# The first projection's accumulating transfers issued at once, the order of the start, and a shorter tail, in a one-core encoder layer

## The chip, the cores and the metric

The kernel runs on one core of a Trainium2 chip. The metric is the device time of one execution in microseconds (us); the time before is the median of three runs.

TensorE (PE in the profile) multiplies and transposes, VectorE (DVE), ScalarE (ACT) and GpSimd (POOL) work element by element, and SyncE (SP) only issues DMA transfers. ACT and POOL issue some as well. Each engine runs its own instructions in order, and semaphores order the engines among each other. PSUM, into which PE writes, has eight banks here, taken from one pool (`ps`).

## The reference, cut to what matters

One layer of a bidirectional encoder, in float32, for one sequence of 512 tokens of 2048 numbers:

```python
h = rmsnorm(x, attn_norm_w[l])
proj = h @ w_in[l]
aq, ak, av, gq, gk, gv, gr, glr = jnp.split(proj, split_idx, axis=-1)
attn = mixture_of_dilations(heads(aq), heads(ak), heads(av), rel_bias_table)
gla_out = gated_linear_attention(gq, gk, gv, glr, gr)       # in both directions
x = x + jnp.concatenate([attn, gla_out], axis=-1) @ w_out[l]
h = rmsnorm(x, ffn_norm_w[l])
x = x + (jax.nn.silu(h @ w_gate[l]) * (h @ w_up[l])) @ w_down[l]
return rmsnorm(x, final_norm_w)
```

`w_in` has 6176 columns, of which the first 2048 give the attention's queries and keys (`aq`, `ak`); the hidden width of the last part is 5632. The final `rmsnorm` multiplies each row by the reciprocal root of its mean square plus 1e-6, and by a weight for each column.

## The kernel before, in words

**Arithmetic.** Every float32 operand is cut into a high part (a cast to fp32r, on ACT) and a low part (the rest, a subtraction on DVE). A product is three matmuls into one bank: high by high, high by low, low by high. The large projections save one in eight block products by a scheme of seven products over sums of blocks of the weights and of the activations; DVE makes these sums (L1399 to L1401), ACT casts them (L1412) and DVE takes the rests (L1417).

**Order of the work.** `run` at the end goes through a list of jobs, each a group of matmuls with a stream of weights (`st`) that is loaded by SP (L209), cast (L237, ACT) and subtracted (L218, DVE). Job 0 begins with `start0` (L1124 to L1159 and around): SP issues the first parts of x and of the weights; ACT issues the attention norm's weights (`wrow1`, L433) and then the identity (`idn`, L434); PE spins on a zero tile (`spin`, L1124), transposes the norm weights by the identity (L1154), spins twice, transposes the first block of x (`prep(0)`, L450, followed by ACT L455), and spins once. The first real matmuls are L346 to L348. Two jobs compute the attention's values. Then `Front.run` computes queries and keys, and the next job computes the gated part's q and k (its first matmul is L337). The attention itself, the rest of the gated part, `w_out`, the feed-forward part (`Feed`), `Down` and the last rows (`finish`) follow.

**Front.** `Front` (L1636 to L1691) has 8 units of 256 output columns, alternately of queries and keys; a unit has 4 pieces of 512 rows of weights, so 32 pieces in all. For each piece it loads weights ahead (`load`), casts and subtracts (`split`), makes the sums of the pieces one and two ahead (`sums`), and runs the seven products on PE (`products`, L1494 and L1508), each into a bank of its own: seven banks for a unit of the eight there are. After the fourth piece `evac7` (L1524 to L1561) reads the seven banks and combines them: ACT copies (L1534 to L1542) into narrow buffers `t`, `r1`, `r2`, `r3` and the result `c`, and DVE adds and subtracts (L1528, L1529). The function is a generator. Up to its first `yield` it runs in the unit's last piece; the rest is put into a queue (`urgent`) from which `run_urgent` takes one step per piece. So one piece later come a wide add (L1552, recorded under L1528) and the four transfers on POOL's queue that add `r1`, `r2` and both halves of `r3` into `c` in memory (L1554 to L1557); the third waits for the first two. Three pieces after that (seven for the last but one unit) `finish` scales `c` by the tokens' reciprocal norms (L1651, DVE) and POOL stores it to `qkd` (L1652). The last unit's scaling is held back (`self.late`).

**Buffers.** Wide buffers (`s4`, 33 of them, names with b) and narrow ones (`s2`, 36, names with a) are handed out first in, first out. Whoever writes into a buffer waits until its last reader, a DMA included, is done. While Front runs, few are free: five narrow ones, all of which `evac7` takes, so that each unit gets the same five in the same roles.

**Around the seam.** In the last unit, Front loads the next job's first weights (`st.load`), after its second piece issues the eight transfers that read the first queries and keys back (`read_qk(0)`, L568, on POOL) and after its third the loads of the gated part's small operands. The next job's weights are cast (L237) when that job starts, behind the last unit's copies on ACT.

**Tail.** `last` (L2061 to L2094) handles the last 512 columns of the last 128 rows in two halves of 256: matmuls, the residual add (L2073, DVE), the sum of squares (L2077, ACT) and the product with the final weight (L2078, DVE). Behind the first half, DVE sums the four earlier partial sums of squares (L2080, L2081). Behind the second, ACT computes logarithm and exponential for the reciprocal root (L2082, L2083), DVE corrects it by one Newton step (L2084 to L2088), and DVE and ACT scale the four output tiles (L2092, L2089), each of which is written by a DMA (L2093) on SP's or ACT's queue.

Of the kernel before, what the change touches and what calls it, by code (L numbers as in the profile page):

```python
# [18 lines left out]
AF = mybir.ActivationFunctionType  # L19
OP = mybir.AluOpType  # L20
# [3 lines left out]
P = 128  # L24
D = 2048
# [6 lines left out]
EPS = 1e-6  # L32
# [80 lines left out]
def put(*slots):  # L113
    for s in slots:
        if s.home is not None:
            s.home.free.append(s.i)


def layer(nc, tc, x, attn_norm_w, w_in, rel_table, gw_f, gb_f, gw_b, gb_b, gla_norm_w, w_out,
# [3 lines left out]
    w_gate, w_up, w_down, out = w_gate[0], w_up[0], w_down[0], out[0]  # L123
# [3 lines left out]
    with tc.manual_schedule(), \  # L127
# [303 lines left out]
        dve.memset(warm, 0.0)  # L431
        xt[0] = [s4.get(F32, [P, 4, 256]) for _ in range(2)]
        act.dma_start(out=wrow1, in_=attn_norm_w[0].rearrange("(r c) -> r c", c=P))  # L433
        act.dma_start(out=idn, in_=c_idn)  # L434

# [75 lines left out]

        def squares(c, t, tiles, ss):
            junk = s2.get()
            act.activation(junk.t, tiles[t].t, AF.Square, accum_out=ss[:, t * 4 + c:t * 4 + c + 1])
            put(junk)
# [611 lines left out]
        def start0():  # L1127
# [27 lines left out]
            dve.tensor_copy(wcol[:, 0:16], b.t)  # L1155
            put(b)
            spin(2)
            prep(0)
            spin(1)  # L1159

# [262 lines left out]
        class Feed(Blocks):  # L1423
# [5 lines left out]
            PRODUCTS = (("R", 0, "B11"), ("Z", 2, "T2"), ("Z", 1, "T1"), ("Z", 0, "T3"), ("R", 2, "B21"),  # L1429
                        ("R", 1, "T4"), ("Z", 3, "B22"))  # L1430
            NARROW = ((0, 0), (1, 0), (2, 0), (2, 1), (0, 1), (3, 1), (3, 0))

# [91 lines left out]
            def evac7(self, u, banks):  # L1524
# [25 lines left out]
                put(*banks)  # L1550
                yield
                add(c[:, 256:768], c[:, 256:768], v.t)  # L1552
# [5 lines left out]
                put(r1, r2, r3)  # L1558
                for _ in range(3 if u < len(self.units) - 2 else 7):
                    yield  # L1560
# [75 lines left out]
        class Front(Feed):  # L1636


            def __init__(self):
# [21 lines left out]
            def run(self):  # L1661
                banks = {}
                for i, (u, q) in enumerate(self.seq):
# [9 lines left out]
                    while 2 * q + 1 not in xi:  # L1673
                        run_side(1)
                    self.products(i, banks[u])
                    if u == len(self.units) - 1:
# [4 lines left out]
                        if q == 2:  # L1681
                            gla_operands()
                    done = None
                    if q == self.per - 1:
                        if u == len(self.units) - 1:
                            s2.free.rotate(14)
                        done = self.evac7(u, banks.pop(u))
                        next(done)
                    run_urgent()
                    if done:  # L1690
                        urgent.append(done)  # L1691

# [334 lines left out]

        def load_wf():
            for c in range(4):
                t = s2.get()  # L2030
                src = final_norm_w[c * 512:(c + 1) * 512].rearrange("(o c) -> o c", o=1)
                pool.dma_start(out=t.t, in_=src.to_broadcast([P, 512]))
                wf.append(t)

        def finish():
# [25 lines left out]
            def last(ys):  # L2061

                t, c = 3, 3
                m, r = scr[0][:, 0:1], scr[1][:, 0:1]
                pre, q = scr[0][:, 1:2], scr[1][:, 1:2]
                sm, sq = sum2[:, t:t + 1], scr[0][:, 2:3]
                junk = s2.get()
                x_ = x1[c][t].t
                for h in range(2):
# [5 lines left out]
                    put(b)  # L2075
                    acc = (ss2[:, 4 * t + 3:4 * t + 4], sq)[h]
                    act.activation(junk.t[:, cols], x_[:, cols], AF.Square, accum_out=acc)  # L2077
                    dve.tensor_tensor(ys[c].t[:, cols], x_[:, cols], wf[c].t[:, cols], op=OP.mult)  # L2078
                    if h == 0:
                        dve.tensor_reduce(sm, ss2[:, 4 * t:4 * t + 4], op=OP.add, axis=mybir.AxisListType.X)  # L2080
                        dve.tensor_scalar(pre, sm, 1.0 / D, EPS, op0=OP.mult, op1=OP.add)  # L2081
                act.activation(q, sq, AF.Ln, scale=1.0 / D, bias=pre)  # L2082
                act.activation(r, q, AF.Exp, scale=-0.5)  # L2083
                dve.scalar_tensor_tensor(m, sq, 1.0 / D, pre, op0=OP.mult, op1=OP.add)  # L2084
                dve.scalar_tensor_tensor(q, r, r, m, op0=OP.mult, op1=OP.mult)
                dve.tensor_scalar(q, q, -0.5, 1.5, op0=OP.mult, op1=OP.add)
                rs = rstdf[:, t:t + 1]
                dve.tensor_tensor(rs, r, q, op=OP.mult)  # L2088
                act.activation(ys[2].t, ys[2].t, AF.Copy, scale=rs)  # L2089
                for c in (0, 2, 1, 3):  # L2090
                    if c != 2:
                        dve.tensor_scalar(ys[c].t, ys[c].t, rs, None, op0=OP.mult)  # L2092
                    (act if c >= 2 else sp).dma_start(out=out[t * P:(t + 1) * P, c * 512:(c + 1) * 512], in_=ys[c].t)  # L2093
                put(junk)  # L2094

            def run():
                for t in range(4):
                    ys = []
                    for c in range(4):
# [7 lines left out]
                        residual(c, t, b)  # L2107
                        squares(c, t, x1[c], ss2)
                        if t == 3:
# [53 lines left out]
```

## Time and profile before

| | us |
|---|---|
| Median of three runs | 2182.22 (2181.07 to 2182.69) |
| The profiled execution's own time | 2181.53 |
| Its span | 2179.8 |
| TensorE busy | 2161.3 (99%) |
| VectorE busy | 1771.2 (81%) |
| ScalarE busy | 1195.9 (55%) |
| GpSimd busy | 338.9 (16%) |

The page gives busy times, the chain of work that ended last and the costliest groups of instructions. Views of the trace show single stretches: a timeline has start and duration of an instruction (or of several of one kind in a row, with their count), the engine, the line, what it writes and reads, and in square brackets how long the engine stood idle before it and what released it. A landing time is what passes from the issue of a transfer until its data is there. Times in rows count from the span's start. Front runs from about 107 us to 267 us, its units 19 to 21 us each.

### The profile page before, as it was taken

What the parts mean: (1) busy time and instruction counts of PE and PEld (TensorE: products, weight loads), DVE (VectorE), ACT (ScalarE), POOL (GpSimd) and SP (SyncE); (2) the same over time, 40 slices, a digit from 0 to 9 for tenths busy, and PEclk for the clock granted to TensorE, in tenths of its full rate; (3) what the DMA queues carried; (4) which work ended last, traced back from release to release, by engine and by line L of the source; (5) the groups of instructions that cost most, each with busy time, mean ns of one, the idle gap of its engine ahead of it and who ended that gap; (6) DMA issues with size and microseconds to landing.
All of it is one profiled execution on the core that took longest, in us unless ns stands there. A gap on an engine that the chain in (4) does not pass through costs nothing.

```text
span 2179.8 us, 34563 instructions
## 1 busy us (share of the span) xinstructions
PE 2161.3 (99%) x12618; PEld 1904.2 (87%) x12618; DVE 1771.2 (81%) x3073; ACT 1195.9 (55%) x2189; POOL 338.9 (16%) x474
## 2 busy tenths in 40 slices
PE   9999999999999999999999999999999999999998
PEld 7888878888888888988888888888888899999986
DVE  5698767776766557899999898998999888898885
ACT  7445456776554335555555555555555655555562
POOL 0011231110011110012212122121221220021300
PEclk9999999999999999999999999999999999999999
DMA  6376774543337873377767777677776975576982
GB/s 201 125 187 173 189 226 141 176 140 111 105 103 270 288 247 107 120 182 177 198 176 183 180 176 196 178 181 182 177 196 176 263 201 182 181 183 157 283 304 78
DMA packets 256856, 397.81 MB, mean 183 GB/s; under 512 B 18925, under 2 KB 154269, under 8 KB 256686
## 3 DMA queue, kind: packets, MB, share of 16 engines
q1 hardware_dynamic: 201262, 272.43, 39.3%
q0 software_dynamic: 54960, 122.58, 24.9%
q8 instruction: 99, 1.62, 0.3%
q14 instruction: 71, 0.58, 0.1%
q10 hardware_dynamic: 464, 0.60, 0.1%
HBM read 285.37 MB, written 64.29 MB: 160 GB/s over the span
## 4 chain that ended last, share of the span: by engine, by line
PE 89%; issue 6%; DMA 2%; DVE 2%; ACT 1%; POOL 0%; ACTq 0%; DVEq 0%; POOLq 0%
PE ps L1508 27%; PE ps L1494 14%; PE ps L346 6%; PE ps L347 6%; PE ps L348 6%; PE ps L1864 5%; PE ps L1865 5%; PE ps L1863 5%; PE ps L339 3%; PE ps L337 3%; PE ps L338 3%; DMA b<-a 2%; PE ps L662 1%; PE ps L1086 1%; PE ps L630 1%
## 5 line engine op out<-in xcount | busy, mean ns | idle before, releaser
L1412 ACT CAST b<-b 128x768 fp32r<-128x768 f32 (+1 forms) x537 | 489.4, 945 | 338.5 <-DVE b L1417 151.2
L1417 DVE TENSOR_TENSOR b<-b,b 128x768 fp32r<-128x768 f32 (+1 forms) x537 | 563.6, 1084 | 32.9 <-ACT b L1412 21.5
L1508 PE MATMUL ps<-b,b 128*128 128x512 f32 x1552 | 451.4, 393 | 0.4 <-ACT b L1412 0.2
L1508 PE MATMUL ps<-a,b 128*128 128x512 f32 x1248 | 366.0, 394 | 3.3 <-DVE b L1528 3.3
L1508 PEld LDWEIGHTS ps<-b,b 128*128 128x128 f32 x1552 | 263.5, 188 | 30.6 <-ACT b L1412 0.7
L1494 PEld LDWEIGHTS ps<-b,b 128*128 128x128 f32 x1552 | 253.1, 190 | 35.8
L1494 PE MATMUL ps<-b,b 128*128 128x256 f32 x1552 | 275.6, 280 | 0.0
L1494 PEld LDWEIGHTS ps<-a,b 128*128 128x128 f32 x1248 | 208.1, 189 | 34.1 <-DVE b L1417 0.5
L1508 PEld LDWEIGHTS ps<-a,b 128*128 128x128 f32 x1248 | 207.2, 189 | 23.3 <-ACT a L1540 4.0
L1494 PE MATMUL ps<-a,b 128*128 128x256 f32 x1248 | 223.8, 281 | 0.0
L1399 DVE TENSOR_TENSOR b<-b 128x512 f32<-128x512 f32 x244 | 167.2, 685 | 17.8 <-DMA b<-in_w_down_dram 7.0
L1864 PE MATMUL ps<-b,b 128*128 128x256 f32 x624 | 176.8, 283 | 0.0
L1863 PE MATMUL ps<-b,b 128*128 128x256 f32 x624 | 176.8, 283 | 0.0
L1865 PE MATMUL ps<-b,b 128*128 128x256 f32 x624 | 176.8, 283 | 0.0
L346 PE MATMUL ps<-b,b 128*128 128x512 f32 x352 | 139.8, 397 | 0.3 <-ACT b L455 0.3
L348 PE MATMUL ps<-b,b 128*128 128x512 f32 x352 | 137.6, 391 | 0.0
L347 PE MATMUL ps<-b,b 128*128 128x512 f32 x352 | 137.5, 391 | 0.0
L1865 PEld LDWEIGHTS ps<-b,b 128*128 128x128 f32 x624 | 119.9, 192 | 0.0
L1863 PEld LDWEIGHTS ps<-b,b 128*128 128x128 f32 x624 | 119.9, 192 | 0.0
L1864 PEld LDWEIGHTS ps<-b,b 128*128 128x128 f32 x624 | 119.9, 192 | 0.0
L218 DVE TENSOR_TENSOR b<-b,b 128x512 fp32r<-128x512 f32 x143 | 95.9, 686 | 26.1 <-ACT b L237 26.0
L1401 DVE TENSOR_TENSOR b<-b,b 128x256 f32<-128x256 f32 x244 | 103.8, 425 | 8.4
(296 smaller groups left out, 4351.7 us busy)
## 6 DMA issues: line engine op xcount, KB each, us to landing
b<-in_w_gate_dram SPq DMA_DIRECT2D x109, 512.0 KB, 3.9
b<-in_w_up_dram SPq DMA_DIRECT2D x88, 512.0 KB, 3.7
b<-in_w_down_dram SPq DMA_DIRECT2D x88, 512.0 KB, 5.9
b<-in_w_in_dram SPq DMA_DIRECT2D x78, 512.0 KB, 4.0
b<-a POOLq DMA_DIRECT2D x150, 256.0 KB, 4.6
b<-in_w_out_dram SPq DMA_DIRECT2D x32, 512.0 KB, 6.6
gd<-b POOLq DMA_DIRECT2D x22, 512.0 KB, 3.9
b<-gd SPq DMA_DIRECT2D x22, 512.0 KB, 5.6
```

What stands on the lines that cost most here:

```text
L346: mm(o, xh.t[:, c], wh.t[:, w], start=first and not on, stop=False, skip_group_check=on)
L347: mm(o, xh.t[:, c], wl.t[:, w], start=False, stop=False, skip_group_check=on)
L348: mm(o, xl.t[:, c], wh.t[:, w], start=False, stop=last, skip_group_check=on)
L1399: dve.tensor_tensor(s_[:, :, 0:2], r[:, :, 1:3], r[:, :, 0:1].to_broadcast(shape), op=OP.add)
L1401: dve.tensor_tensor(s_[:, :, 3], s_[:, :, 2], r[:, :, 3], op=OP.add)
L1412: act.copy(o, src)
L1417: dve.tensor_tensor(o, src, h, op=OP.subtract)
L1494: mm(o, wl, xh, start=False, stop=end, skip_group_check=True)
L1508: mm(o.rearrange("p (s t) -> p s t", s=2), wh, x_, start=first and p == 0, stop=False, skip_group_check=True)
L1863: mm(o, xh[:, t], wh, start=first and h == 0, stop=False, skip_group_check=True)
L1864: mm(o, xh[:, t], wl, start=False, stop=False, skip_group_check=True)
L1865: mm(o, xl[:, t], wh, start=False, stop=last, skip_group_check=True)
```

## The change

At the start ACT issues the identity ahead of the norm weights, and one spin stands before the first transposes instead of two, two behind them instead of one.

In Front (`early = True`; `Feed` keeps its order) the wide add and the four accumulating transfers follow the copies and adds of `evac7` at once, without a step in between. The scaling and the store of a unit come when piece `min(i + 6, 31)` is reached, where i is the unit's last piece; the last unit's stays held back. In the last piece of the last unit, before its products are issued, `st.split` casts the next job's first two weight tiles and takes their rests, so that these stand on ACT ahead of the last unit's copies.

In the tail the sums of squares of the last rows go to one row of a small tile that also holds the constant for epsilon (set by a POOL memset in `load_wf`). ACT sums them with an accumulating copy behind the first half. Behind the second half, DVE multiplies and sums in one instruction, ACT computes logarithm and exponential with the total as bias, the Newton step ends with two factors instead of their product, and DVE scales all four tiles with both, their writes going to SP and ACT in turn.

```diff
         dve.memset(warm, 0.0)
         xt[0] = [s4.get(F32, [P, 4, 256]) for _ in range(2)]
+        act.dma_start(out=idn, in_=c_idn)
         act.dma_start(out=wrow1, in_=attn_norm_w[0].rearrange("(r c) -> r c", c=P))
-        act.dma_start(out=idn, in_=c_idn)
 
         rb = {}
         hT = {}
...
             pe.transpose(b.t, wrow1, idn[0:16, 0:16])
             dve.tensor_copy(wcol[:, 0:16], b.t)
             put(b)
+            spin(1)
+            prep(0)
             spin(2)
-            prep(0)
-            spin(1)
 
         def between0(i, b):
             if i == 0 and b == 1:
...
+            early = False
...
                 add(c[:, 768:1024], t1[:, a], v.t[:, z])
                 add(c[:, a], m2[:, a], t.t[:, a])
                 put(*banks)
-                yield
+                if not self.early:
+                    yield
                 add(c[:, 256:768], c[:, 256:768], v.t)
                 put(t, v)
                 pool.dma_start(out=c[:, 0:512], in_=r1.t, accum_op=OP.add)
...
                 pool.dma_start(out=c[:, 256:768], in_=r3.t, accum_op=OP.add)
                 pool.dma_start(out=c[:, 768:1024], in_=r3.t[:, z], accum_op=OP.add)
                 put(r1, r2, r3)
-                for _ in range(3 if u < len(self.units) - 2 else 7):
+                for _ in range(1 if self.early else 3 if u < len(self.units) - 2 else 7):
                     yield
                 yield from self.finish(u, c_, c)
 
...
         class Front(Feed):
 
+            early = True
 
             def __init__(self):
                 self.units = [(w_in, c + g * 256) for g in range(4) for c in (C_AQ, C_AK)]
...
-                banks = {}
+                banks, ends = {}, deque()
                 for i, (u, q) in enumerate(self.seq):
                     banks.setdefault(u, [])
                     self.load()
...
                         st.load()
                     while 2 * q + 1 not in xi:
                         run_side(1)
+                    if u == len(self.units) - 1 and q == 3:
+                        st.split(jobs[n_front].first + 2)
                     self.products(i, banks[u])
                     if u == len(self.units) - 1:
                         for p in (2 * q, 2 * q + 1):
...
                             read_qk(0)
                         if q == 2:
                             gla_operands()
-                    done = None
                     if q == self.per - 1:
                         if u == len(self.units) - 1:
                             s2.free.rotate(14)
                         done = self.evac7(u, banks.pop(u))
                         next(done)
+                        ends.append((min(i + 6, 31) if u < 7 else 99, done))
                     run_urgent()
-                    if done:
-                        urgent.append(done)
+                    while ends and ends[0][0] <= i:
+                        for _ in ends.popleft()[1]:
+                            pass
+                urgent.append(ends.pop()[1])
 
         fr = Front()
 
...
+            pool.memset(ss1[:, 4:5], EPS * D)
             for c in range(4):
                 t = s2.get()
...
-                m, r = scr[0][:, 0:1], scr[1][:, 0:1]
-                pre, q = scr[0][:, 1:2], scr[1][:, 1:2]
-                sm, sq = sum2[:, t:t + 1], scr[0][:, 2:3]
+                sq, total = ss1[:, 16:17], ss1[:, 17:18]
+                m, r, q = ss1[:, 18:19], ss1[:, 19:20], ss1[:, 15:16]
                 junk = s2.get()
                 x_ = x1[c][t].t
                 for h in range(2):
...
                     dve.scalar_tensor_tensor(x_[:, cols], b.t[:, cols], rstd2[:, t:t + 1], x_[:, cols],
                                              op0=OP.mult, op1=OP.add)
                     put(b)
-                    acc = (ss2[:, 4 * t + 3:4 * t + 4], sq)[h]
-                    act.activation(junk.t[:, cols], x_[:, cols], AF.Square, accum_out=acc)
+                    if h == 0:
+                        act.activation(junk.t[:, cols], x_[:, cols], AF.Square, accum_out=ss1[:, 3:4])
+                        act.activation(ss1[:, 8:13], ss1[:, 0:5], AF.Copy, scale=1.0 / D, accum_out=total)
+                        dve.tensor_tensor(ys[c].t[:, cols], x_[:, cols], wf[c].t[:, cols], op=OP.mult)
+                        continue
+                    dve.tensor_tensor_reduce(junk.t[:, cols], x_[:, cols], x_[:, cols], 1.0 / D, 0.0,
+                                             op0=OP.mult, op1=OP.add, accum_out=sq)
+                    act.activation(q, sq, AF.Ln, bias=total)
+                    act.activation(r, q, AF.Exp, scale=-0.5)
+                    dve.tensor_tensor(m, sq, total, op=OP.add)
                     dve.tensor_tensor(ys[c].t[:, cols], x_[:, cols], wf[c].t[:, cols], op=OP.mult)
-                    if h == 0:
-                        dve.tensor_reduce(sm, ss2[:, 4 * t:4 * t + 4], op=OP.add, axis=mybir.AxisListType.X)
-                        dve.tensor_scalar(pre, sm, 1.0 / D, EPS, op0=OP.mult, op1=OP.add)
-                act.activation(q, sq, AF.Ln, scale=1.0 / D, bias=pre)
-                act.activation(r, q, AF.Exp, scale=-0.5)
-                dve.scalar_tensor_tensor(m, sq, 1.0 / D, pre, op0=OP.mult, op1=OP.add)
-                dve.scalar_tensor_tensor(q, r, r, m, op0=OP.mult, op1=OP.mult)
+                dve.scalar_tensor_tensor(q, r, m, r, op0=OP.mult, op1=OP.mult)
                 dve.tensor_scalar(q, q, -0.5, 1.5, op0=OP.mult, op1=OP.add)
-                rs = rstdf[:, t:t + 1]
-                dve.tensor_tensor(rs, r, q, op=OP.mult)
-                act.activation(ys[2].t, ys[2].t, AF.Copy, scale=rs)
-                for c in (0, 2, 1, 3):
-                    if c != 2:
-                        dve.tensor_scalar(ys[c].t, ys[c].t, rs, None, op0=OP.mult)
-                    (act if c >= 2 else sp).dma_start(out=out[t * P:(t + 1) * P, c * 512:(c + 1) * 512], in_=ys[c].t)
+                for c in range(4):
+                    o = ys[c].t
+                    dve.tensor_scalar(o, o, r, q, op0=OP.mult, op1=OP.mult)
+                    (sp, act)[c % 2].dma_start(out=out[t * P:(t + 1) * P, c * 512:(c + 1) * 512], in_=o)
                 put(junk)
...
-                        squares(c, t, x1[c], ss2)
+                        squares(c, t, x1[c], ss2 if t < 3 else ss1[:, 0:4], 0 if t == 3 else 4 * t)
```

5 lines of the change are left out of this document (3 added, 2 removed).

## The prediction

> **What bounds the kernel now.** I read the page first: TensorE (PE) is busy for nearly the whole span, so time can only come from moments when it stands still.
>
> ```profile
> span 2179.8 us, 34563 instructions
> ...
> PE 2161.3 (99%) x12618; PEld 1904.2 (87%) x12618; DVE 1771.2 (81%) x3073; ACT 1195.9 (55%) x2189; POOL 338.9 (16%) x474
> ```
>
> The profiled execution took 2181.53 us, 1.73 outside its span; the sum below is made against it. Next, PE's waits (line, what it waited for, total us, times, longest):
>
> ```profile
> PE ps L1508 <- DVE b L1528: 3.5, 5, 1.7
> PE ps L1154 <- DMA idn<-in_c_idn_dram: 1.3, 1, 1.3
> ...
> PE ps L337 <- ACT b L237: 1.3, 1, 1.3
> ```
>
> These are the first projection (five waits for a bank that DVE has not yet read out), the start, and the seam between the first projection and the next job. The diff touches all three, and the tail. The waits do not hold the pipeline's refill, so I take the loss in the first projection from PE's timeline (start, us, engine, line). The first and third row are the same place in a unit, one unit apart; the second is the step that follows it undisturbed, the last the same step three units later, behind its wait:
>
> ```profile
> 167.08 0.40 PE L1494 MATMUL ps<-a,b 128*128 128x256 f32 x2
> 167.31 0.40 PE L1508 MATMUL ps<-a,b 128*128 128x512 f32 x1
> ...
> 186.57 0.40 PE L1494 MATMUL ps<-a,b 128*128 128x256 f32 x2
> ...
> 249.44 0.70 PE L1508 MATMUL ps<-a,b 128*128 128x512 f32 x2 [0.77 <-DVE b L1528]
> ```
>
> An undisturbed unit takes 186.57 - 167.08 = 19.49 us. From 186.57 to 249.44 pass 62.87 us, of which 3 x 19.49 = 58.47 are work, and 0.23 is the ordinary step (167.31 - 167.08). Lost: 62.87 - 58.70 = **4.17 us** at four unit boundaries. The three boundaries before 167 lose nothing.
>
> **Part 1, the transfers of a unit issued at once.** One round of the loop that causes the loss, from the timelines of ACT, DVE and POOL:
>
> ```profile
> 185.21 0.37 ACT L1535 COPY a<-ps 128x256 f32<-128x256 f32 x1 [4.10 <-DMA b<-a]
> ...
> 192.01 0.69 DVE L1528 TENSOR_TENSOR b<-b,a 128x512 f32<-128x512 f32 x1
> ...
> 201.72 1.21 POOL L1557 DMA_DIRECT2D b<-a  x1
> ...
> 205.51 0.37 ACT L1535 COPY a<-ps 128x256 f32<-128x256 f32 x1 [4.37 <-DMA b<-a]
> ```
>
> L1535 fills r3. The wide add comes 192.01 - 185.21 = 6.80 us later, a piece late, behind the next sums. Then 205.51 - 192.01 = 13.50 us pass until the last accumulating transfer out of r3 has landed and the next unit's L1535 may overwrite it (only five narrow buffers are free here, so r3 always gets the same one). The round is 20.30 us against 19.49 of matmuls, so each unit falls 0.81 behind: nothing at first, while there is slack, then a stall at every boundary. The change puts add and transfers straight behind the copies. How soon that can be shows the last boundary, where no transfer delays ACT:
>
> ```profile
> 264.35 0.37 ACT L1535 COPY a<-ps 128x256 f32<-128x256 f32 x1 [1.02 <-PE ps L1494]
> ...
> 267.14 0.37 ACT L1541 COPY b<-ps 128x256 f32<-128x256 f32 x1
> ```
>
> The add needs L1541's result: 267.51 - 264.35 = 3.16 us behind L1535. The new round is 3.16 + 13.50 = 16.66 us, 2.83 below 19.49. The waits for the transfers go, and with them all 4.17 us: **-4.2**. The scaling (L1651, 1.2 us) and the store move six pieces on, where they sit between DVE's sums. What is late next is DVE:
>
> ```profile
> 146.00:166.00 20.00, 20.00 (x117) 17.59 (x116) 18.18 (x29) 9.86 (x18) 4.08 (x5) 1.00 0.74 178
> ```
>
> In this stretch without stalls (columns behind the length: PE, PEld, DVE, ACT, POOL busy, granted clock, DMA share, GB/s) DVE works 18.18 of 20 us, 17.7 of 19.49. The new place of the add makes DVE wait for L1541 with the next piece's sums, subtractions and so the next weights queued behind it: some 0.9 us a unit (two copies like L1541, 0.37 each, and the step between engines), 18.6 in all. It fits, with under 1 us left, so I count nothing. From 1.8 us of waiting a unit DVE would be the bound; at 2.0 PE loses 0.2 a unit, 1.5 us over seven units, which I take as that end.
>
> **Part 2, the seam.** The next job's first two weight tiles are now cast on ACT ahead of the last unit's nine copies.
>
> ```profile
> 266.71 0.39 PE L1494 MATMUL ps<-b,b 128*128 128x256 f32 x2
> 268.35 0.50 PE L337 MATMUL ps<-b,b 128*128 128x512 f32 x1 [1.25 <-ACT b L237]
> ```
>
> Today PE starts L337 1.64 us after 266.71, where 0.23 is usual: 1.41, and with the slow refill right behind it about **1.8 us** lost. If both casts could run freely, all of that would go. The first can: its buffer is that of weights whose products are done. The second takes, by the order of the pool, the buffer of unit 5's result, free only when that unit's store (L1652) has landed; and the store now stands on POOL behind the eight reads of q and k (L568). Behind the waiting cast on ACT stand all copies of the last unit, and behind these the banks that PE needs. POOL at this place before, the landing times of L1652 and then of L568 (min/median/max):
>
> ```profile
> 262.49 1.21 POOL L1557 DMA_DIRECT2D b<-a  x1
> 263.04 3.81 POOL L568 DMA_DIRECT2D a<-qkd  x6
> 268.13 0.52 POOL L568 DMA_DIRECT2D a<-qkd  x1 [1.29 <-DMA b<-a]
> 272.18 0.52 POOL L568 DMA_DIRECT2D a<-qkd  x1 [3.52 <-DMA b<-a]
> ```
> ```profile
> DMA to landing us min/median/max: 2.9/3.1/6.5
> ```
> ```profile
> DMA to landing us min/median/max: 2.5/5.2/13.0
> ```
>
> The last two rows wait for transfers that were issued eight before them, L1556 and L1557; the store, next in line behind the eighth read, will wait in the same way for the first read to land. On the clock of before: L1535 of unit 6 undelayed at 264.35 - 19.49 = 244.86, its add at 248.0, L1557 by 9.7 us later (201.72 - 192.01) at 257.7, the reads from 258.3. With L1557 landing in about 4 to 5 us (205.51 - 201.72 = 3.8 inside the first projection; 9.7 us in the rows above, where 262.49 goes with 272.18) the eighth read goes out at 262 to 263; the first read, at its median, lands at 263.5; the store goes out at 263.6 and lands 3.1 to 6.5 later, at 266.7 to 270.1. ACT's first copies are needed near 263 and the last bank PE can do without is gone some 2 us later (an estimate from 264.35 and the two copies behind it), so PE stalls from a landing after about 264.9: 1.8 to 5.2 us. I take 3.0, nearer the median landing: **+1.2** against the 1.8 of before. The ends are -1.8 (no wait) and, with L1557 9.7 us late as in the rows above (eighth read at 267.4, store at 268, landing 271 to 274.5), 6 to 9.6 lost, +4.2 to +7.8.
>
> The reads of q and k go out 4.7 us sooner, and ACT's wait for them and a PE wait behind it shorten:
>
> ```profile
> 274.11 0.63 ACT L591 ACTIVATE a<-a 128x512 fp32r<-128x512 f32 x1 [3.64 <-DMA a<-qkd]
> ```
> ```profile
> 290.73 0.51 PE L339 MATMUL ps<-b,a 128*128 128x512 f32 x1 [0.29 <-DVE a L218]
> ```
>
> With the scaling and wide add of the last unit no longer in between, I count the second row as gone: **-0.3**. Later buffers get other numbers, with the same counts in the same order: 0, between -1 and +1 (the nearest rows are single waits of 0.3 to 1.3 us).
>
> **Part 3, the start.** The chain of waits, and the landing time of L433 (min/median/max):
>
> ```profile
> 0.74 0.46 ACTq L433
> ...
> 1.23 3.48 DMA idn<-in_c_idn_dram
> ...
> 4.84 0.26 PE ps L1154
> 5.10 1.15 PE ps L1124 x4
> ...
> 8.68 0.43 PE ps L347
> ...
> 10.85 0.23 PE ps L348
> ```
> ```profile
> DMA to landing us min/median/max: 2.4/2.4/2.4
> ```
>
> The identity is issued one instruction sooner, 1.23 - 0.74 = 0.49 us; the norm weights behind it, at 1.23 + 2.4 to 3.48, land by 4.7 at the latest. One spin instead of two ahead of the first transposes saves half of 1.15, 0.57; the second spin behind them gives back about 0.2, as it ends after ACT has the operand ready. Together **-0.9** (0.4 if the norm weights land last, 1.4 at best). But a matmul takes 0.43 at 8.68 and 0.23 at 10.85: the clock comes up in between. If it comes up at the same moment, what is done sooner is done at half speed, and only 0.5 of the 0.9 is left: +0.4 on the total. [...]
>
> **Part 4, the tail.**
>
> ```profile
> 2170.17 0.17 DVE small L2080
> ...
> 2170.52 0.40 DVE a L2073
> ...
> 2170.94 0.52 ACT a L2077 x2
> ...
> 2172.49 0.17 DVE small L2088
> ...
> 2172.68 0.48 DVE a L2092
> ```
> ```profile
> DMA to landing us min/median/max: 2.3/3.0/3.8
> ```
> ```profile
> 294.19 0.69 DVE L640 CUSTOM_DVE_ANT_0 a<-ps,b 128x512 f32<-128x512 f32 x1
> ```
>
> L2080 and L2081 no longer stand ahead of the last residual: 0.3 us. The squares (ACT, 0.52 with its read-out) become a multiply-reduce on DVE; its kin of 512 columns takes 0.69, so 256 cost 0.4 to 0.7, taken 0.5: nothing. L2088 falls away: 0.19. The scaling starts 0.5 sooner, but DVE now does all four, so the last output leaves 0.1 to 0.2 sooner only. The landing times (before: L2093, 2.3 to 3.8) grow from the first to the last of four writes, so they queue for the write path, and its start counts: **-0.5** (0.1 to 0.6).
>
> **Sum.** -4.2 + 1.2 - 0.3 - 0.9 - 0.5 = -4.7: 2176.8 us. The runs' median, 2182.22, lies 0.7 above the profiled execution, so I forecast **2177.5 us**. About 0.2% (4.4 us) can be told from no change.
>
> **The rivals.**
> - *Clean seam.* The store has landed in time (a 2.5 us read, a 2.9 us store: 257.7 + 0.6 + 3.8 + 0.6 + 2.9 = 265.6): stall 0.7 or none. 2174.5 to 2175.2. For it: the store's median is near its minimum. Against: three transfers must land in turn. 0.2.
> - *Crowded seam.* L1557 lands as late as at 272: +4.2 to +7.8 instead of +1.2, 2180.5 to 2184. For it: the only rows of these reads directly behind L1557 at this place. Against: they start 4.7 us earlier, with other traffic. 0.2.
> - *Slower than before.* The same queue, but the first read itself lands after its longest, 13.0: 258.3 + 13.0 = 271.3, store 6.5 later, 277.8, stall 12.9, net +11.1 against 5.9 of gains: 2187.4. It decides from a landing after 264.9 + 1.8 + 5.9 = 272.6. 0.06.
> - *The first projection still waits* (DVE is the bound, or the earlier transfers meet the weight loads and land 3 us later, which eats the 2.83): 1.7 to 4.2 of the gain stays out, 2179.2 to 2181.7. 0.12.
> [...]
>
> **How the numbers follow.** The forecast's case (2175.8 to 2179) has 0.42. Faster by over 0.2% means below 2177.9: the clean seam and most of the forecast's case, and some of the rest: 0.58. Slower by over 0.2% (above 2186.6): 0.05. Within: 0.37. The range 2173.0 to 2182.0 runs from the clean seam with 1.5 us of unknowns to the middle of the crowded one.
>
> **What would show it.** Right: ACT's L1535 waits no more for a transfer, and PE's waits for L1528 go; units take 19.5 us throughout. At the seam, the second of L237's casts waits for a transfer (a store, qkd) with the copies behind it, and PE stands some 3 us. At the start L347 stands near 7.8 instead of 8.68; at the end the output scaling begins 0.5 us sooner behind the last matmul. Wrong: waits at L1535 that stay; DVE busy without a gap and PE waiting for weights; a seam without a wait, or with over 6 us.

## The result and the profile after

The changed kernel takes 2192.56 us (median of six runs) against 2181.64 us for the kernel before in the same comparison: a ratio of 1.0053, with a 95% interval of 1.0041 to 1.0066. It is slower by about 11 us where 4.7 us less were forecast. The profiled execution's span is 2191.2 us. Medians here and below are of undisturbed executions; of `store_first` (below) two of eight took 4402 and 7645 us and are left out.

The page of the changed kernel, first, for the same two rows as before:

```profile
span 2191.2 us, 34554 instructions
...
PE 2167.7 (99%) x12618; PEld 1905.7 (87%) x12618; DVE 1771.9 (81%) x3073; ACT 1195.1 (55%) x2188; POOL 338.6 (15%) x475
```

The share of PE is the same, and its busy time has even grown by 6.4 us for the same 12618 matmuls: part of the loss lies in matmuls that ran slower, not in waits (some 3 us of it at the seam, below). The waits of PE (line, what it waited for, total us, times, longest; the diff moved line numbers by a few, so L1508 is L1510 here, L1154 is L1155, L1528 is L1530):

```profile
PE ps L337 <- DVE a L1530: 3.9, 1, 3.9
PE ps L1510 <- DVE a L1530: 3.8, 4, 1.0
PE ps L1510 <- DVE b L1530: 1.8, 5, 0.4
PE ps L1155 <- DMA wrow<-in_attn_norm_w_dram: 1.3, 1, 1.3
```

All the stretches that the change touched still have their wait, and the seam has a longer one. Who keeps DVE, on which PE waits, shows in DVE's own waits, and for the seam in ACT's:

```profile
DVE b L1400 <- DMA qkd<-b: 14.7, 5, 3.2
```
```profile
ACT b L237 <- DMA qkd<-b: 11.1, 1, 11.1
```

Both wait for a store to `qkd`. In the kernel before, ACT's waits for the accumulating transfers were the cause, in its list of waits:

```profile
ACT a L1535 <- DMA b<-a: 24.6, 6, 5.5
```

These are gone in the changed kernel, as forecast, and the two waits for a store stand in their place.

**Inside the first projection.** One round of the new loop, from the timelines of DVE and POOL (L1557 to L1560 are the four accumulating transfers, L1655 the scaling, L1656 the store):

```profile
183.69 0.69 DVE L1400 TENSOR_TENSOR b<-b 128x512 f32<-128x512 f32 x1 [3.12 <-DMA qkd<-b]
...
198.21 1.22 DVE L1655 TENSOR_TENSOR b<-b,a 128x1024 f32<-128x1024 f32 x1
...
205.71 0.69 DVE L1400 TENSOR_TENSOR b<-b 128x512 f32<-128x512 f32 x1 [2.75 <-DMA qkd<-b]
```
```profile
191.85 0.86 POOL L1557 DMA_DIRECT2D b<-a  x1 [13.72 <-DVE b L1400]
192.41 1.21 POOL L1558 DMA_DIRECT2D b<-a  x1
198.59 0.87 POOL L1559 DMA_DIRECT2D b<-a  x1 [4.97 <-DMA b<-a]
199.13 1.21 POOL L1560 DMA_DIRECT2D b<-a  x1
199.73 1.17 POOL L1656 DMA_DIRECT2D qkd<-b  x1
```

The same place in the kernel before, where the store (L1652 there) goes out ahead of the next unit's transfers (L1554 is the first):

```profile
188.87 0.56 POOL L1652 DMA_DIRECT2D qkd<-b  x1 [6.54 <-DVE b L1651]
193.32 0.86 POOL L1554 DMA_DIRECT2D b<-a  x1 [3.88 <-DVE b L1399]
```

The store of a unit now goes out 1.1 and 0.6 us behind the next unit's third and fourth accumulating transfer. It has landed by 205.71, 6.0 us later. The buffer that it frees goes to the sums of a later piece; DVE, in order, stands still until then, and with it the subtractions, the next weights and the evacuation of the banks. A round is 205.71 - 183.69 = 22.02 us against 19.49 of matmuls, longer than the 20.30 of before. The landing times of the stores (min/median/max) were 2.9/3.1/6.5 before; now:

```profile
DMA to landing us min/median/max: 2.9/6.1/6.7
```

The trace's packet records show which part of the landing grew. A transfer is moved in packets; those of a store have 4096 bytes here, those of an accumulating transfer 2048 or 1024. In the first five units the first packet of the store follows its issue by 1.1 us in the kernel before and by 2.6 to 4.0 us now. For the store issued at 199.73 it comes at 203.16, when 124 of the 128 packets of the third transfer and 21 of the fourth's are done. So the store mostly waits to begin; once begun, this one moved in 2.1 us, against 1.6 before (190.01 to 191.62).

**At the seam.** ACT, POOL and PE of the changed kernel:

```profile
264.95 0.61 ACT L237 CAST b<-b 128x512 fp32r<-128x512 f32 x1
276.62 0.62 ACT L237 CAST b<-b 128x512 fp32r<-128x512 f32 x1 [11.06 <-DMA qkd<-b]
277.15 0.36 ACT L1536 COPY a<-ps 128x256 f32<-128x256 f32 x1
```
```profile
265.02 4.83 POOL L569 DMA_DIRECT2D a<-qkd  x8
269.85 0.57 POOL L1656 DMA_DIRECT2D qkd<-b  x1
```
```profile
273.61 0.40 PE L337 MATMUL ps<-b,b 128*128 128x512 f32 x1
273.84 0.39 PE L338 MATMUL ps<-b,b 128*128 128x512 f32 x1
274.07 0.39 PE L339 MATMUL ps<-b,b 128*128 128x512 f32 x1
278.35 0.79 PE L337 MATMUL ps<-b,b 128*128 128x512 f32 x1 [3.89 <-DVE a L1530]
278.95 0.63 PE L338 MATMUL ps<-b,b 128*128 128x512 f32 x1
```

The second cast waits 11 us for a store that left at 269.85, behind eight reads, and landed some 6.7 us later; the nine copies stand behind the cast. PE runs three matmuls into its one free bank and then has none: from 274.07 to 278.35 it loses 4.28 - 0.23 = 4.05 us. Behind that the same matmul takes 0.43 us (from one L338 or L339 to the next) instead of 0.23, until about 284: the clock has fallen. The profile records it as the granted clock, the share of TensorE's full speed; in this row (length; busy PE, PEld, DVE, ACT, POOL; granted clock; DMA share; GB/s) it is 0.50:

```profile
277.55:280.96 3.41, 2.61 (x6) 2.02 (x7) 3.11 (x9) 3.41 (x12) 0.00 (x0) 0.50 1.01 399
```

From 278.35 to 284.54 PE makes 14 steps of its matmuls, which take 14 x 0.23 = 3.2 us at full clock and 6.2 here: another 3.0 us.

**Where the 11.5 us between the two spans come from**, by the start of the same matmul in both traces: start +0.3; first projection +6.4 (its last products stand 273.38 - 266.71 = 6.67 later, the start included); seam -1.8, then +4.05 for the stall and +3.0 for the slow matmuls; some 0.4 in small steps; the tail -0.9.

### The profile page after: what moved, and what is told of

It is laid out like the page before. It is cut to its first block, busy times and chain, and to the rows that moved or that the text cites. A ratio compares the mean times of both kernels' runs of the same rounds, so it can differ in the third digit from the quotient of the medians.

```text
span 2191.2 us, 34554 instructions
## 1 busy us (share of the span) xinstructions
PE 2167.7 (99%) x12618; PEld 1905.7 (87%) x12618; DVE 1771.9 (81%) x3073; ACT 1195.1 (55%) x2188; POOL 338.6 (15%) x475
## 4 chain that ended last, share of the span: by engine, by line
PE 85%; DVE 2%; issue 1%; DMA 1%; ACT 0%; POOL 0%; DVEq 0%; ACTq 0%; POOLq 0%
PE ps L1510 24%; PE ps L1496 12%; PE ps L346 5%; PE ps L348 5%; PE ps L347 5%; PE ps L1872 5%; PE ps L1873 5%; PE ps L1871 5%; PE ps L339 3%; PE ps L337 3%; PE ps L338 3%; PE ps L663 1%; PE ps L1087 1%; PE ps L631 1%; PE ps L688 1%
## 5 line engine op out<-in xcount | busy, mean ns | idle before, releaser
L1510 PE MATMUL ps<-b,b 128*128 128x512 f32 x1552 | 451.0, 393 | 0.4 <-ACT b L1413 0.2
L1510 PE MATMUL ps<-a,b 128*128 128x512 f32 x1248 | 366.4, 394 | 6.6 <-DVE a L1530 3.8
L1510 PEld LDWEIGHTS ps<-b,b 128*128 128x128 f32 x1552 | 263.5, 188 | 30.7 <-ACT b L1413 0.7
L1510 PEld LDWEIGHTS ps<-a,b 128*128 128x128 f32 x1248 | 207.2, 189 | 28.3 <-DVE a L1530 4.6
L1400 DVE TENSOR_TENSOR b<-b 128x512 f32<-128x512 f32 x244 | 167.4, 686 | 32.2 <-DMA qkd<-b 14.7
L1872 PE MATMUL ps<-b,b 128*128 128x256 f32 x624 | 176.6, 283 | 0.0
L346 PE MATMUL ps<-b,b 128*128 128x512 f32 x352 | 140.0, 398 | 0.0
L218 DVE TENSOR_TENSOR b<-b,b 128x512 fp32r<-128x512 f32 x143 | 95.9, 685 | 34.5 <-ACT b L237 34.4
L1872 PEld LDWEIGHTS ps<-b,b 128*128 128x128 f32 x624 | 119.8, 192 | 0.0
L1557 POOL DMA_DIRECT2D b<-a x50 | 43.2, 865 | 439.4 <-ACT b L1413 237.4
```

What stands on the lines that cost most here:

```text
L218: dve.tensor_tensor(h[3].t, raw.t[:, h[1] * 512:(h[1] + 1) * 512], h[2].f, op=OP.subtract)
L346: mm(o, xh.t[:, c], wh.t[:, w], start=first and not on, stop=False, skip_group_check=on)
L1400: dve.tensor_tensor(s_[:, :, 0:2], r[:, :, 1:3], r[:, :, 0:1].to_broadcast(shape), op=OP.add)
L1510: mm(o.rearrange("p (s t) -> p s t", s=2), wh, x_, start=first and p == 0, stop=False, skip_group_check=True)
L1872: mm(o, xh[:, t], wl, start=False, stop=False, skip_group_check=True)
```

## The experiments

**Theory Q** (queue): the store stands behind the next unit's accumulating transfers on POOL's queue and so lands late, and the buffer it frees is waited for, in the units by DVE and at the seam by ACT. **Rivals:** D, DVE has no room left for the add's wait for the copies; L, the two pieces of further delay are what hurts; S, the loss comes from the seam or the start. All are compared with runs of the kernel before on the same chip: 2182.72 us for front_only, seam_only, store4 and store_first, 2182.12 for the other four.

### One part alone: front_only, seam_only, ends_only

*front_only*: the kernel before with the edits of `evac7`, `ends` and `early` alone, without these lines:

```diff
-                    if u == len(self.units) - 1 and q == 3:
-                        st.split(jobs[n_front].first + 2)
```

> The kernel before with only the first projection's edit: add and accumulating transfers at once, scaling and store six pieces on; no early cast at the seam, old start, old tail. Theory Q (the store of a unit now stands on POOL behind the next unit's accumulating transfers, lands some 6 us after its issue, and DVE's next sums wait for the buffer that it frees; the round closes at 22.0 us a unit): DVE's L1400 waits for a store in five units, about 14.7 us in all, the units from the fourth on last 22.0 us, and the seam's first matmul stands 5 us later than before; the seam's own 1.8 us stay, with up to 2 more where the second weight half waits for its store, and TensorE's clock does not fall. Time 2186.5 to 2189. Rival D (DVE is the bound because the add waits in order for the copies): the same loss, but DVE waits for ACT and not for a transfer. Rival S (the loss in the first projection comes from the early start or the seam): 2178.

Measured: 2193.52 us, ratio 1.0048 (1.0036 to 1.0060). Its waits of DVE:

```profile
DVE b L1399 <- DMA qkd<-b: 17.6, 5, 4.3
```

The wait is for a transfer, in five units, as Q has it, and not for ACT (D). S falls: this one part costs as much as the whole change. The loss is larger than expected (2186.5 to 2189): 9.3 us in the first projection where the changed kernel had 6.4; the rounds last 22.3 to 23.2 us, with the stores' landing at 6.5 in the median. Two runs below that have the first projection of the changed kernel unaltered lose 8.2 (split1) and 8.7 us (warm_seam) there, so this loss scatters from profile to profile; why was not followed up. And the clock did fall, against the expectation: it stood at half from 279.35 to 282.76, behind a wait at the seam of 1.3 us and one of 0.9.

*seam_only*: the kernel before with only the two lines above added.

> The kernel before with only the two early casts at the seam. Here the store of unit 5 leaves before the reads of q and k, and the second cast's buffer is another one. Theory Q: the 11 us wait of ACT for a store is gone, PE starts the next job 0.2 us behind the last product, 1.8 us are regained and the clock stays: 2179.5 to 2180.5. Rival (two casts and their rests ahead of the copies hold up the banks anyway): the seam still loses 1.5 us or more, 2181 to 2183.

Measured: 2180.98 us, ratio 0.9991 (0.9983 to 1.0000). Here unit 5's store has long landed, both casts run, and PE goes through the seam without a gap:

```profile
258.11 1.14 ACT L237 CAST b<-b 128x512 fp32r<-128x512 f32 x2
```
```profile
266.55 0.39 PE L1494 MATMUL ps<-b,b 128*128 128x256 f32 x2
266.77 0.40 PE L337 MATMUL ps<-b,b 128*128 128x512 f32 x1
```

L337 follows 0.22 behind and stands 1.58 us sooner than before. The 1.8 us at the seam are regained, as Q has it; the time alone lies between the ranges of Q and of the rival. The early casts are good by themselves; the late store spoils them.

*ends_only*: the kernel before with only the start and the tail of the change.

> The kernel before with only the start (identity first, spins the other way round) and the tail. The tail alone gives 0.5 to 0.9 us. At the start the norm weights land last, the first matmul comes 0.4 to 0.9 us sooner, and what is left of it at full speed hangs on when the clock comes up: between 0.3 us lost and 1 gained. [...] Rival (the start's full gain of the forecast): under 2180.5.

Measured: 2180.15 us, ratio 0.9989 (0.9980 to 0.9997): a little faster, and by the time alone within the rival's range. The trace splits it: the tail, from the start of the last matmul to the span's end, is 9.03 us against 9.91. The start gains nothing in this profile: the first L346 stands at 7.63 instead of 7.88, but PE's matmuls come to full speed only at 11.2 instead of 10.5 us, and the sixtieth matmul is 0.3 later. PE waits 1.5 us at L1155 for the weights that now come second. Over all profiles the start looks better; that is taken up below.

### Delay or queue: store4, store_first, store_sp

*store4* takes two pieces of delay away and leaves the order of issue as it is:

```diff
-                        ends.append((min(i + 6, 31) if u < 7 else 99, done))
+                        ends.append((min(i + 4, 31) if u < 7 else 99, done))
```

> The changed kernel with min(i + 4, 31) in place of min(i + 6, 31): the scaling and the store come two pieces sooner, as long behind the copies as in the kernel before, but still after the next unit's four transfers in the order of the program. Theory Q: what counts is the place on POOL, so the store leaves no sooner (behind the third and fourth transfer, which wait for the first two), but its buffer is wanted two pieces sooner: DVE waits 6 to 7 us a unit instead of 3, a round takes 28 to 29 us, and the time is 2225 to 2240. Rival L (the two pieces of delay are what hurts): DVE's waits go, and the time is 2174 to 2180.

Measured: 2224.43 us, ratio 1.0194 (1.0179 to 1.0209), just under the expected range. DVE's waits:

```profile
DVE b L1400 <- DMA qkd<-b: 52.5, 6, 9.8
```

The sooner the store is due and the buffer given back, the worse: the wait is 8.8 us a unit, because the store still stands behind the third transfer, and this waits for the first two to land. One store whose scaling ends at 201.90 leaves only at 208.61. A round is 27.7 us (L1400 behind its wait at 186.51 and at 214.24). L would have it faster than before; it falls.

*store_first* has the scaling and the store four pieces behind the unit's last, as store4 has, and changes the order: copies and narrow adds, then the scaling and store of the unit before, then the wide add and the transfers.

```diff
-                if not self.early:
-                    yield
+                yield
                 add(c[:, 256:768], c[:, 256:768], v.t)
...
                         next(done)
-                        ends.append((min(i + 6, 31) if u < 7 else 99, done))
+                        if ends:
+                            for _ in ends.popleft():
+                                pass
+                        next(done)
+                        ends.append(done)
                     run_urgent()
-                    while ends and ends[0][0] <= i:
-                        for _ in ends.popleft()[1]:
-                            pass
-                urgent.append(ends.pop()[1])
+                urgent.append(ends.pop())
```

> The changed kernel with the scaling and the store of a unit issued behind the copies and narrow adds of the next unit and ahead of its wide add and transfers. Theory Q: the store leaves before the transfers, lands in about 3 us, no sum waits for it; the transfers still leave 4 to 5 us sooner than in the kernel before, so that the copies wait for none: the first projection loses under 0.5 us, the seam nothing, 2174 to 2176.5. Rival D (DVE has no room for the add's wait in order): a loss of 1 to 2 us a unit stays, 2180 to 2188.

Measured: 2177.03 us, ratio 0.9972 (0.9961 to 0.9983): faster than both kernels, half a microsecond above the expected range. POOL's timeline and DVE's waits:

```profile
185.34 0.56 POOL L1655 DMA_DIRECT2D qkd<-b  x1 [9.80 <-DVE b L1654]
186.26 0.86 POOL L1556 DMA_DIRECT2D b<-a  x1 [0.35 <-DVE b L1400]
```
```profile
DVE b L1400 <- DMA qkd<-b: 2.1, 6, 0.5
```
```profile
262.18 0.40 PE L337 MATMUL ps<-b,b 128*128 128x512 f32 x1
```

The eight units take 156.0 us from the first matmul of the first projection to L337, 8 x 19.5: nothing is lost at any boundary or at the seam. That is 4.2 us less than before in the first projection, just what was forecast for it. The stores, now only 0.9 to 1.3 us ahead of the transfers, land in 4.0 to 4.3 us in the first six units, not in the expected 3, and that is soon enough. L337 stands 6.17 us sooner than before. D falls with it: DVE has the room. What this kernel gives back later (4.5 us between the spans, not 6.2 and a tail) goes into small new waits, the longest 1.1 us at L1872.

*store_sp* leaves the order of the program as it is and sends the store by another queue:

```diff
-                    pool.dma_start(out=qkd[u], in_=c)
+                    sp.dma_start(out=qkd[u], in_=c)
```

> The changed kernel with one word changed: the stores of the units to qkd go out on SP's queue, nothing else moves. Theory Q: a store no longer stands behind the next unit's third and fourth transfer; it leaves right behind the scaling, some 1.5 to 4 us sooner, and lands before DVE's sum wants its buffer: L1400 waits under 3 us in all, the first projection's stalls go, and the second cast at the seam finds its buffer free. 2174.5 to 2178. Rival (it is the six pieces, or the transfers at once, that hurt, wherever the store stands): 2188 to 2193.

Measured: 2180.33 us, ratio 0.9990 (0.9981 to 0.9999). The store, and the landing times as far as the trace has them (two of the eight stores):

```profile
195.70 0.34 SPq L1656 DMA_DIRECT2D qkd<-b  x1
```
```profile
DMA to landing us min/median/max: 2.8/3.3/3.7
```

It leaves as late as before behind its scaling (195.70, scaling from 194.46: 1.24 us; in the changed kernel 199.73 - 198.21 = 1.52) and amid the same two accumulating transfers (195.49 and 196.03), yet this one lands in 2.8 us, not 6.0. The packets tell of the others: in the first five units the first packet follows the issue by 0.8 to 1.8 us (changed kernel 2.6 to 4.0) and the last is through after 2.4 to 5.2 (5.5 to 6.0). So what made the store late in the changed kernel was above all its place in the queue behind those two; that it takes up to 5.2 us here too shows a smaller share of the traffic. The expectation that it would leave 1.5 to 4 us sooner was wrong, L1400 waits 4.7 us in all where under 3 were expected, and the second cast at the seam still waits 3.3 us, without holding PE up. Of the 4.2 us forecast for the first projection 3.6 are gained and 0.6 lost; L337 stands 5.0 us sooner than before. The total misses the expected 2174.5 to 2178, since a new wait takes most of it back:

```profile
269.38 0.71 ACT L804 CAST a<-a 128x256 fp32r<-128x256 f32 x2 [4.66 <-DMA a<-in_w_in_dram]
```
```profile
266.54 0.39 PE L339 MATMUL ps<-b,b 128*128 128x512 f32 x1
270.39 0.66 PE L811 MATMUL ps<-b,a 128*64 128x512 f32 x1 [3.46 <-DVE a L805]
270.84 0.63 PE L812 MATMUL ps<-b,a 128*64 128x512 f32 x1
```

The operands of L811 had not come in: PE, now 5 us early, is ahead of a load that SP issues at 260.28 and that lands 9 us later. In store_first the same load left at 258.20 and held PE up by under 1 us. SP now also waits in order for the scalings (47.7 us in seven waits) with its loads behind them; whether this delayed the load was not tested. Again the stall (3.6 us) is followed by matmuls at 0.43.

### Stall and clock: split1, warm_seam

*split1* casts only one weight tile ahead of the copies:

```diff
-                        st.split(jobs[n_front].first + 2)
+                        st.split(jobs[n_front].first + 1)
```

> The changed kernel with one early cast at the seam instead of two. The buffer of unit 5's result then goes to the last unit's result, so ACT's sixth copy waits for the same store, with three banks or so already read. Theory Q with the clock: PE goes on for about 9 matmuls (2 us) and then stands 2 to 3 us instead of 4.05, too short for the clock to fall, so the 13 matmuls at half speed behind it go as well: 2187 to 2190. Rival (the seam's loss is only the casts ahead of the copies): the stall goes altogether, 2185 to 2186. Rival (the clock falls after any stall): 2.7 us more.

Measured: 2192.20 us, ratio 1.0045 (1.0032 to 1.0057); missed. That a stand of 2 to 3 us would be too short for the clock to fall was an estimate that no run shows; in front_only it had fallen behind waits of 1.3 and 0.9 us. As expected PE gets nine matmuls far (three in the changed kernel), but then stands in several pieces, and the clock falls all the same, later:

```profile
277.54 0.47 PE L337 MATMUL ps<-b,b 128*128 128x512 f32 x1 [1.33 <-DVE b L1530]
...
280.42 0.51 PE L339 MATMUL ps<-b,a 128*128 128x512 f32 x1 [0.94 <-DVE a L218]
...
282.39 0.63 PE L812 MATMUL ps<-b,a 128*64 128x512 f32 x1
282.82 0.63 PE L811 MATMUL ps<-b,a 128*64 128x512 f32 x1
```

No single step between two matmuls here is longer than 1.71 us, in 5.5 us (275.83 to 281.36) with six matmuls. The seam costs 3.8 us here, 1.5 less than in the changed kernel; the total hides it, since this run's first projection lost 8.2 us, not 6.4.

What stands ahead of the fall, if no single long gap does? The granted clock stood at half for 3.41 us in front_only (279.35 to 282.76) and in warm_seam, below (210.35 to 213.76), and for 6.83 us in the changed kernel (277.55 to 284.37). Two stretches of 3.41 us of split1 (columns as in the row of the changed kernel's seam) show how little PE was busy in all:

```profile
278.31:281.72 3.41, 1.77 (x6) 0.76 (x6) 3.38 (x7) 3.41 (x8) 1.82 (x2) 1.00 1.03 396
281.72:285.13 3.41, 3.41 (x10) 2.00 (x9) 3.33 (x6) 1.73 (x4) 0.00 (x0) 0.50 1.05 344
```

PE was busy 1.77 of 3.41 us, and in the next stretch the clock is at 0.50. In the changed kernel's stall it was 0.33 of 3.42 (274.13 to 277.55, with 0.50 behind it), in the kernel before at the seam, where the clock held at 1.00, 2.16 of 3.41 (266.28 to 269.69). So the short waits of split1 together go with a fall as the one long stall does; how little of PE's work it takes, these three stretches do not tell.

*warm_seam* fills the stall with matmuls of zeros that nobody reads:

```diff
                 fr.run()
+                spin(20)
```

> The changed kernel with 20 spins on the zero tile (some 4.3 us of PE time at full clock) between the first projection and the next job, where PE stood still for 4.05 us; they change no result. Clock theory (the half speed behind the stall comes from PE's idleness): the matmuls behind the stall take 0.23 us at once, 2.6 us are regained, less 0 to 1 us for the three matmuls that came before the stall: 2189 to 2192. Rival (the slow matmuls come from something else, as reads of the same memory): they stay at 0.43 us, 2192 to 2194.

Measured: 2194.00 us, ratio 1.0050 (1.0037 to 1.0064).

```profile
274.52 4.63 PE L1125 MATMUL ps<-warm 128*128 128x128 f32 x40
279.70 0.50 PE L337 MATMUL ps<-b,b 128*128 128x512 f32 x1 [0.55 <-DVE a L1530]
280.03 0.39 PE L338 MATMUL ps<-b,b 128*128 128x512 f32 x1
280.26 0.40 PE L339 MATMUL ps<-b,b 128*128 128x512 f32 x1
```

L338 follows L337 and L339 follows L338 at 0.33 and 0.23: the slow matmuls are gone, so they came from PE's idleness; the granted clock stays at 1.00 through the seam. The time lies in the rival's range all the same, for two reasons. The spins took the free bank, the first matmuls came behind them at 279.70 instead of 273.61 and then waited bank by bank (0.3 to 0.6 us three times): the seam costs 5.4 us, where it cost 5.3 without spins. And this run's first projection lost 8.7 us, not 6.4; there the clock fell once, from 210.35 to 213.76, behind a stretch of 3.41 us in which waits left PE busy for 0.83 us. At the seam the clock was kept; the time was not won.

## Why the prediction was wrong, point by point

- **The step that failed:** "The scaling (L1651, 1.2 us) and the store move six pieces on, where they sit between DVE's sums." I priced this move on DVE alone, at nothing. The store's place on POOL's queue was not looked at there: before, it left ahead of the next unit's transfers (store at 188.87, the transfers from 193.32); now it leaves behind them, lands in 6 us instead of 3, and its buffer is wanted two pieces behind the scaling in both kernels. -4.2 was forecast, +6.4 came. "Six pieces on" counts from the unit's last piece; against the kernel before, where the store already stood four pieces behind it, the move is two pieces. The transfers came one piece sooner at the same time, and already by this they stand ahead of the store; store4, which undoes the two pieces alone, is worse. That the order decides was shown by store_first (0 lost) and store_sp (0.6 lost), against store4.
- The forecast that **ACT's waits for the accumulating transfers go** was right, and so was the loop that bound the kernel before: with the store out of the way the units ran at 19.5 us and the 4.2 us were gained (store_first). "I count nothing" for DVE's room was right too.
- **The seam:** the chain cast, store, reads was right, only its size was not. +1.2 net was forecast, with a stall of 3.0; 5.3 came (-1.8 + 4.05 + 3.0), within the crowded rival's 4.2 to 7.8, but by another way. POOL's eight reads did not wait (265.02, eight in 4.83 us); the store simply left behind them and took some 6.7 us to land. And the sum had no term for the clock: the stall of 4 us is followed by matmuls at 0.43, which cost the 3.0.
- **The wait at 290** stayed as it was (L339 behind L218, 0.3).
- **The start:** -0.9 was forecast, +0.3 measured. "0.4 if the norm weights land last" was the case: L1155 starts at 4.91 and waits for `wrow`. What was sooner was done at half speed (0.43 us from one matmul to the next, later 0.23), and full speed came later:

```profile
10.67 0.63 PE L348 MATMUL ps<-b,b 128*128 128x512 f32 x1
11.10 0.49 PE L346 MATMUL ps<-b,b 128*128 128x512 f32 x1
11.43 0.40 PE L347 MATMUL ps<-b,b 128*128 128x512 f32 x1
```

  Full speed begins at 11.4 us here, 10.5 before, and in the other profiles between 9.3 and 11.2, whichever start they had. The clock is recorded as up at 11.31 us here, at 10.28 in the kernel before, and in all ten profiles between 8.7 and 11.3. The +0.3 is this profile's own: in the seven profiles with the new start the first L346 stands at 7.0 to 7.6 us, in the three with the old one at 7.9 to 8.5: 0.9 sooner in the mean, the size that was forecast. But the moment of full clock does not follow, and at the sixtieth matmul the new start is 0.55 sooner in the mean, where single profiles scatter over 1.6 us: about the 0.5 that part 3 leaves of the 0.9 should the clock come up at the same moment. That it does, no run shows: the moment scatters over 2.6 us.
- **The tail:** -0.5 was forecast, -0.9 came. The scaling begins 2184.58 - 2182.21 (the last matmul's start) = 2.37 us behind the last matmul, where it was 2.84, as worked out. That the four writes queue for a write path was an estimate from landing times that the kernel before has at 2.3 us for the first and 3.8 for the last; no run tested it. The rest lies in the writes, whose end scatters: the tail was 9.5 to 10.0 us in three profiles with the old one, 8.8 to 9.3 with the new.

```profile
2184.58 1.92 DVE L2099 TENSOR_SCALAR a<-a,ss 128x512 f32<-128x512 f32 x4
```

- **Slower than before** had 0.06 and hung on one landing at the seam alone. The same wait, a buffer held by a store behind other transfers, could act in every unit; that case was not among the rivals.

## What to carry to other kernels

When an edit moves a transfer, list what stands ahead of it on its own queue and who gets the buffer that it frees, in every round of the loop and not only at the place that looks risky; a store that used to land in 3 us takes 6 behind two accumulating transfers. When a loop closes over a buffer, write its round as a sum of durations for the old and the new order (20.30, 22.02 and 27.7 us here, against 19.49 of work): that says at once which one wins. And where an edit lets PE stand, in one stall or in several short waits, count the slow matmuls behind it as well (in the changed kernel 14 steps of 0.43 us instead of 0.23, 3.0 us).

## What the hardware showed unexpectedly

- A store issued on POOL right behind two accumulating transfers landed in 5.9 to 6.4 us (first five units); alone on that queue, before, in 3.1 to 4.0. Issued as late behind its scaling, but on SP's queue, its packets were through after 2.4 to 5.2 us, against 5.5 to 6.0 on POOL's.
- After 4.05 us (changed kernel) and 3.6 us (store_sp) lost in a stall, matmuls took 0.43 us instead of 0.23 for 3 to 6 us. With several shorter waits, none over 1.71 us, within 5.5 us (split1) it happened too. With spins in the gap (warm_seam) it did not.
- The granted clock fell to 0.50 behind 3.41 us in which PE was busy for 1.77 (split1, in several short waits), and held at 1.00 behind 3.41 us with 2.16 (the kernel before, at the seam).
